# Attention values projected with 512 moving columns in place of 256

## The chip, the cores and the metric

One core of a Trainium2 chip runs the whole network in one launch. The metric is device time in microseconds. The engines are TensorE (PE, with its weight loads apart as PEld), VectorE (DVE), ScalarE (ACT), GpSimd (POOL) and SyncE (SP), which issues most DMAs here.

## The reference, cut to what matters

Four residual layers with token mixers A, B, C, A, each followed by a dense SwiGLU layer; 512 tokens, 1024 channels, float32. The change lies in mixer C, attention with three head groups of 16 heads (64 channels each) and dilations 1, 4 and 16:

```
qkv = (h @ w_qkv).reshape(b, s, N_ATTN_GROUPS, 3, HEADS_PER_GROUP, HEAD_DIM)
for g, (window, dil) in enumerate(DILATED_GROUPS):
    q = head_rms_norm(qkv[:, :, g, 0], q_gain[g])
    k = head_rms_norm(qkv[:, :, g, 1], k_gain[g])
    v = qkv[:, :, g, 2]
    o, l = dilated_group_attention(q, k, v, bias_g, dil, (window // 2) // dil)
wts = softmax(lses over the groups);  o = sum of wts * outs;  return o @ w_o
```

The values v have no norm of their own; the layer's norm is a factor per token.

## The kernel before, in words

The input of attention lies feature-major, as two float32r parts Hi and Lo whose sum is the value. A large product takes three matmuls per 128 rows of contraction: high by high, low by high, high by low. Weights come as chunks of 128 x 1024 in the order of their use (class Stream): SP loads a chunk into one of three raw buffers; ScalarE copies its high part (line 191), VectorE subtracts to get the low part (line 192), up to two chunks ahead of the use, each into rings of three. Loads wait on SP for a raw buffer, which comes free with the split.

Attention runs over n = 0 to 23: n // 3 is a pair of heads, n % 3 the group g. `gemm_qk(n, 0)` and `gemm_qk(n, 1)` make queries and keys of two heads with 24 matmuls of 512 columns (lines 332 to 334, stationary weights); VectorE scales the result by the norm (line 1397 and neighbours), ScalarE squares, VectorE rounds (line 1406), GpSimd takes the low part of the squares (line 1408). One step later `norms` sums the squares on TensorE (lines 1417, 1418) and ScalarE takes the root; `normed` scales on VectorE (line 1428). `score` (line 1450) follows one step after that, `soft` (VectorE 1464, ScalarE 1469), `divide` (GpSimd 1481), then `transposes` (TensorE 1503, copies out on ScalarE and VectorE 1505) and, four steps after the start, `pv` (TensorE 1518, 1522), the product of probabilities and values.

`gemm_v` makes the values of four heads of one group, tokens on the partitions: here the activations are stationary and the weights move. Group 0 takes 128 tokens in order; groups 1 and 2 take every fourth token, a stationary operand with a stride (`tok`, lines 1350 and 1351). It has four token tiles of 256 columns, two to a PSUM bank, and two weight chunks of four contraction tiles each, 96 matmuls (lines 1375 to 1377) in all. The copies out are two on VectorE (line 1381) and two on ScalarE (line 1383). In the loop it stands at the end of an iteration, for four heads per call: group 0 at n = 2, 8, 14, 20; group 1 at n = 3, 9, 15, 21; group 2 at n = 4, 10, 16 and, for the last heads, in the tail after the loop, before `score(22)`.

```
if 2 <= n < N - 2 and (n - 2) % 6 < 3:
    gemm_v((n - 2) // 6, (n - 2) % 6)
```

Between the parts of an iteration stand four `slot()` calls. Each takes the next closure of a list: after every four heads `merge_weights` (transposes of the logarithms, a softmax over three groups, a round trip through DRAM that copies a row to 64 partitions) and `merge_outputs` (GpSimd scales by these weights, line 1583; VectorE adds, lines 1587 and 1588). The program order within each engine's queue is the order in the code. PSUM has two rings of four banks: `psg` ("pg") for the large products and norms, `pst` ("pt") for scores, transposes and `pv`.

After the loop the last heads' steps are written out by hand, with the output projection (`project`, operand OH) in between.

Of the kernel before, what the change touches and what calls it, by code (L numbers as in the profile page):

```python
# [34 lines left out]
# ---------------------------------------------------------------- host layout  # L35
# [10 lines left out]
def _constants():  # L46
# [18 lines left out]
    # positions 2u and 2u + 1 against the frequencies to 128, and the position 256  # L65
# [39 lines left out]
def _host_arrays(v):  # L105
# [24 lines left out]
    w = v["attn_w_qkv"][0].reshape(KT, P, 3, 3, 4, 256)[:, :, :, 2]  # L130
    w = w.reshape(2, 4, P, 3, 4, 256)
    a["wv"] = cc(w.transpose(4, 3, 0, 2, 1, 5)).reshape(4, 3, 2, P, CH)
# [21 lines left out]
# ---------------------------------------------------------------- the program  # L154
class Stream:
    """Weight chunks in the order of their use. They are loaded ahead into a ring of
    buffers; those of the large products are split into two float32r parts, w = hi + lo
    exactly, one chunk ahead of their use."""
# [6 lines left out]
    def _room(self, tag, free):  # L165
        """Is the buffer that comes next in the ring given back?"""
        r, n = self.rings[tag], WBUFS if tag == "wch" else HBUFS
        return len(r) < n or r[-n] < (self.nsplit if tag == "wch" and self.loaders[r[-n]][1] else free)
# [35 lines left out]
    def next(self, count=1, ahead=True):  # L204
        """The next chunks; those given out before are free."""
        n = self.nuse
        if ahead:
            self.ahead(count)
        else:
            self._load(n)  # L210
        self.nuse += count
        out = [self.tiles.pop(i) for i in range(n, n + count)]
        return out if count > 1 else out[0]


class Net:
# [45 lines left out]
    # ---- weights in order of use  # L262
    def loaders(self):
# [6 lines left out]
        for l, kind in self.plan:  # L270
# [25 lines left out]
            elif kind == "attn":  # L296
                for n in range(24):
                    add(a["wqk"][n // 3, n % 3, 0])
                    add(a["wqk"][n // 3, n % 3, 1])
                    if n >= 2 and (n - 2) % 6 < 3:  # L300
                        v = [a["wv"][(n - 2) // 6, (n - 2) % 6, c] for c in range(2)]
                        if n < 22:
                            for x in v:
                                add(x)
                for x in v:
                    add(x)
                for half, kp in [(h, k) for h in range(2) for k in range(3)] + [(0, 3), (1, 3)]:
                    add(a["wo"][half, kp])
# [5 lines left out]
    def run_bg(self, slots):  # L314
        """Background work, spread over the slots that are left."""
        self.due += len(self.bg0) / self.slots if slots > 1 else len(self.bg0)
        while self.bg and len(self.bg0) - len(self.bg) < self.due:
            self.bg.pop(0)()
# [5 lines left out]
    def keep_warm(self, count):  # L324
        """Matmuls without a use, so that TensorE's clock isn't halved by the wait that follows."""
        ps = self.psg.tile([P, S], F32, name="pg", tag="pg")
        for _ in range(count):
            self.nc.tensor.matmul(ps, self.r[:, 0:P], self.r, start=True, stop=True)
# [7 lines left out]
    def gemm(self, hi, lo, chunk=None, ps=None, ks=range(KT)):  # L336
        """The next chunk's 128 columns against all of hi + lo."""
# [7 lines left out]
    # ---- residual stream and norms  # L345
# [4 lines left out]
    def mirrored(self, m):  # L350
        """Places of H for the positions: those above 256 backwards, 512 - s at 256 + s."""
# [3 lines left out]
    def start(self, nxt):  # L355
        """The first layer's input, as it comes in."""
# [19 lines left out]
    def after_x(self, m, nxt, late=None, defer=False):  # L376
# [38 lines left out]
        else:  # L415
# [5 lines left out]
            if late:  # L421
                # high part on ScalarE; VectorE takes the next sum before it waits for that
# [10 lines left out]
    def next_h(self):  # L433
        """A second place for the next layer's input."""
# [17 lines left out]
    # ---- feed forward  # L452
# [44 lines left out]
    def split_mul(self, hi, lo, t1, t2):  # L497
        """hi + lo = t1 * t2."""
# [5 lines left out]
    # ---- Fourier mixing  # L504
    def fnet(self, l, nxt):
        nc, H, j = self.nc, self.H, l // 3
        with ExitStack() as st:
# [12 lines left out]
            # the positions s = 2u and 2u + 1, then 512 - s for the odd and for the even ones. Position  # L520
            # 256, in the place of 512, is not to be folded: its row is taken apart.
# [6 lines left out]
            # block by block as the input comes in, for the first three tiles of tokens; the last  # L528
            # tile's products then run beside the norm's factors
# [24 lines left out]
            # the factors of the mirrored positions, in their order; zero at the place of 512  # L554
# [10 lines left out]
            def middle(hf, last):  # L565
                """Position 256."""
# [17 lines left out]
            def spread(u, ps, c):  # L584
                """The frequencies above 128 from those below."""
# [30 lines left out]
            def product(m, c):  # L616
                """The mixed channels' product with 128 columns of the weights."""
# [80 lines left out]
    # ---- S5: constants from the parameters, kept in DRAM until layer 1  # L698
# [12 lines left out]
    def store_h(self, k):  # L711
        """Block k of x * gain to DRAM."""
        self.nc.sync.dma_start(self.HB[k], self.H[:, k, :])

    def load_u(self, k):
        """... and back with (channel in group, step in chunk) on the partitions."""
# [3 lines left out]
    def s5_prepare(self):  # L720
        """Closures that each issue a part of the preparation."""
# [52 lines left out]
        def pexp1(x, scale=1.0):  # L774
            """exp(scale * x), to float32's accuracy, begun: x = k ln 2 + r."""
# [44 lines left out]
        def factors1():  # L820
            """(exp(lambda dt) - 1) / lambda."""
# [20 lines left out]
        def factors3():  # L842
            """One chunk's turn back, for the shift of the states."""
# [166 lines left out]
    # ---- S5 mixing  # L1010
# [10 lines left out]
    def s5_phase(self, k):  # L1021
        """The angles' cosines and sines."""
# [6 lines left out]
    def s5(self, l, nxt):  # L1029
# [7 lines left out]
        with self.s5_pools as st:  # L1037
# [10 lines left out]
            # the norm's factors with (channel, step in chunk) on the partitions  # L1048
# [9 lines left out]
            # The chunks of the backward direction are taken in reverse, so that both directions' scans are  # L1058
            # one. 64 chunks and a zero for each group make the groups' scans one, too; their results,
            # a column on, are the states each chunk starts from.  # L1060
# [73 lines left out]
            def spare(k, name, bufs):  # L1134
                """The angles' buffers serve again once their scans are done."""
# [12 lines left out]
            def product(ps, g, yw, k):  # L1148
                """One group's outputs: from the chunk's own inputs and from the state before it."""
# [18 lines left out]
            def outputs(k, half):  # L1168
                """Half of the groups of two blocks, which run beside each other on TensorE's columns."""
# [6 lines left out]
            def outputs1(k):  # L1176
                """The last two blocks, one by one."""
# [9 lines left out]
            def features(k):  # L1187
                """The outputs of blocks k - 1 and k back to feature-major; GELU."""
# [87 lines left out]
    # ---- attention  # L1276
# [5 lines left out]
    def attn_prepare(self):  # L1282
        """Bias rows by offset, copied 128 times so that skewed reads give the bias tiles."""
# [22 lines left out]
        return [load, lambda: None, rows(0), rows(1), rows(2), st.close]  # L1306

# [13 lines left out]
    def attn(self, l, nxt):  # L1321
# [27 lines left out]
        # tile t of 128 tokens: in order for group 0, every fourth token for the others  # L1349
# [3 lines left out]
        def norm_cols():  # L1353
            """The norm's factors with tokens on the partitions."""
# [9 lines left out]
        def gemm_v(q, g):  # L1364
            v = p2.tile([P, 4, 256], F32, name=f"v{g}", tag=f"v{g}", bufs=1)
            pp = [self.psg.tile([P, 2, 256], F32, name="pg", tag="pg") for t in range(2)]
            for c in range(2):
                wh, wl = [t.rearrange("p (k c) -> p k c", k=4) for t in self.stream.next()]
                for t in range(4):
                    ps = pp[t // 2][:, t % 2]  # L1370
                    for k in range(4):
                        kk = 4 * c + k
                        x, y = tok(Hi[:, kk], g, t), tok(Lo[:, kk], g, t)
                        # one start per bank: it clears the whole bank's marks
                        mm(ps, x, wh[:, k], start=(kk == 0 and t % 2 == 0), stop=False, skip_group_check=True)  # L1375
                        mm(ps, y, wh[:, k], start=False, stop=False, skip_group_check=True)  # L1376
                        mm(ps, x, wl[:, k], start=False, stop=(kk == 7), skip_group_check=True)  # L1377
            for t in range(4):
                s = rc[:, int(g > 0), t:t + 1]
                if t < 2:  # L1380
                    V.tensor_scalar(v[:, t], pp[t // 2][:, t % 2], s, None, M)
                else:
                    A.activation(v[:, t], pp[t // 2][:, t % 2], AF.Copy, scale=s)
# [47 lines left out]
        def score(n):  # L1431
# [3 lines left out]
            # (rows, query tile, columns of p, first key)  # L1435
# [10 lines left out]
            # the two heads lie in different rows of the array, and go side by side  # L1446
# [61 lines left out]
        def pv(n):  # L1508
# [4 lines left out]
            for t in range(4):  # L1513
                for h in range(2):
                    hc = slice(64 * (2 * (hp % 2) + h), 64 * (2 * (hp % 2) + h) + 64)
# [13 lines left out]
        def spread(copy, out, ps, g):  # L1529
            """From a group's order of the tokens to theirs."""  # L1530
# [9 lines left out]
        def merge_weights(q):  # L1540
            lr = p2.tile([P, 3, S], F32, name="lr", tag="mrg")[0:4]
            mxx = p2.tile([4, S], F32, name="mxx", bufs=1)
# [49 lines left out]
        # the output projection, in chunks of two k-tiles and four m-tiles  # L1592
# [22 lines left out]
        for n in range(N - 1):  # L1615
# [19 lines left out]
            if 2 <= n < N - 2 and (n - 2) % 6 < 3:  # L1635
                gemm_v((n - 2) // 6, (n - 2) % 6)
        # the last heads, with the output projection's products for the others between them
# [8 lines left out]
        gemm_v(3, 2)  # L1646
# [55 lines left out]
    # ---- all layers  # L1702
# [50 lines left out]
```

## Time and profile before

| | us |
|---|---|
| median of 3 runs (2568.99 to 2569.63) | 2569.31 |
| span of the profiled execution (first to last instruction), its own time as far as the profile gives one | 2565.2 |
| attention, about 1084 to 1786 of the span | 702 |
| one call of `gemm_v`, group 0 | 11.5 |
| one call of `gemm_v`, group 1 or 2 | 22.5 |

The profile has one execution: times are microseconds from the span's start. A matmul's end is modelled, so the spacing of starts tells its cost, not its length. "Idle before" and the releaser say how long an engine stood before an instruction and what ended that.

### The profile page before, as it was taken

Reading aid. Unit: us, or ns where it says so; the run is one execution under the profiler, and the core shown is the slowest. Engines: PE = TensorE matmul, PEld = TensorE weight load, DVE = VectorE, ACT = ScalarE, POOL = GpSimd, SP = SyncE. Lnnn points to the kernel's source line nnn. Section 1 sums busy time; section 2 is a strip of 40 time slices with the busy share of each in tenths; the row PEclk is TensorE's granted clock in tenths of the full one; section 3 lists DMA queues with packets and bytes.
Section 4 is the critical chain, followed back from the end, with each engine's and each line's share of the span. In section 5 each row is a group of like instructions: output and inputs, shape, how many; then the busy total and the mean of one; then the engine's idle time right before and its main releaser. Section 6 shows DMA issues by size and latency. Waiting matters only on the chain.

```text
span 2565.2 us, 31445 instructions
## 1 busy us (share of the span) xinstructions
PE 2446.1 (95%) x12330; PEld 2034.3 (79%) x12330; DVE 1394.7 (54%) x2143; ACT 871.8 (34%) x1515; POOL 629.6 (25%) x496
## 2 busy tenths in 40 slices
PE   9999978968998999999999999989999999999999
PEld 7777756857887787889888797877888888788887
DVE  7669999487542334462754646556433444543332
ACT  3322112434232223342644526354322322332231
POOL 4464554142110001121332323322110112310010
PEclk9999988989999999999999999999999999999999
DMA  4246876683226463322132322313322222222222
GB/s 148 91 138 208 243 208 193 209 287 118 97 102 100 122 128 118 108 75 66 58 91 66 91 66 66 91 50 91 107 99 99 98 93 97 85 96 99 99 98 83
DMA packets 137944, 293.80 MB, mean 115 GB/s; under 512 B 32449, under 2 KB 73508, under 8 KB 137796
## 3 DMA queue, kind: packets, MB, share of 16 engines
q1 hardware_dynamic: 136316, 288.09, 36.8%
q10 hardware_dynamic: 1480, 3.70, 0.5%
q8 instruction: 97, 1.59, 0.3%
q14 instruction: 51, 0.42, 0.1%
HBM read 259.66 MB, written 36.21 MB: 115 GB/s over the span
## 4 chain that ended last, share of the span: by engine, by line
PE 72%; DVE 15%; ACT 5%; DMA 3%; issue 3%; POOL 3%; SPq 0%; ACTq 0%; DVEq 0%; POOLq 0%
PE pg L332 19%; PE pg L334 19%; PE pg L333 19%; DVE wlo L192 3%; PE pg L1377 2%; PE pg L1376 2%; PE pg L1375 2%; DMA w<-in_wdn_dram 1%; ACT whi L191 1%; DMA w<-in_wgu_dram 1%; DVE s5bd L733 1%; ACT p L1469 1%; DVE wout L733 1%; DVE ce L733 1%; DVE ms L1115 1%
## 5 line engine op out<-in xcount | busy, mean ns | idle before, releaser
L192 DVE TENSOR_TENSOR wlo<-w,whi 128x1024 fp32r<-128x1024 f32 x360 | 484.1, 1348 | 613.3 <-ACT whi L191 606.4
L334 PE MATMUL pg<-HH,wlo 128*128 128x512 f32 x1792 | 709.7, 396 | 40.7 <-DVE wlo L192 40.7
L332 PE MATMUL pg<-HH,whi 128*128 128x512 f32 x1792 | 715.0, 399 | 7.9 <-ACT whi L191 4.5
L333 PE MATMUL pg<-HH,whi 128*128 128x512 f32 x1792 | 707.4, 395 | 2.1 <-DVE HH L419 2.1
L191 ACT CAST whi<-w 128x1024 fp32r<-128x1024 f32 x360 | 376.2, 1048 | 583.0 <-PE pg L333 408.6
L334 PEld LDWEIGHTS pg<-HH,wlo 128*128 128x128 f32 x1792 | 342.1, 191 | 118.7 <-DVE wlo L192 46.2
L332 PEld LDWEIGHTS pg<-HH,whi 128*128 128x128 f32 x1792 | 342.8, 191 | 88.0 <-ACT whi L191 5.7
L333 PEld LDWEIGHTS pg<-HH,whi 128*128 128x128 f32 x1792 | 342.4, 191 | 75.2 <-DVE HH L419 4.5
L502 POOL TENSOR_TENSOR act<-t,act 128x512 fp32r<-128x512 f32 x88 | 116.2, 1321 | 937.0 <-ACT act L501 889.3
L332 PE MATMUL pg<-act,whi 128*128 128x512 f32 x704 | 276.1, 392 | 11.0 <-ACT whi L191 10.5
L333 PE MATMUL pg<-act,whi 128*128 128x512 f32 x704 | 275.5, 391 | 1.6 <-POOL act L502 1.6
L334 PE MATMUL pg<-act,wlo 128*128 128x512 f32 x704 | 275.3, 391 | 0.0
L332 PEld LDWEIGHTS pg<-act,whi 128*128 128x128 f32 x704 | 132.9, 189 | 40.7 <-ACT whi L191 10.9
L333 PEld LDWEIGHTS pg<-act,whi 128*128 128x128 f32 x704 | 133.0, 189 | 30.4 <-POOL act L502 3.0
L334 PEld LDWEIGHTS pg<-act,wlo 128*128 128x128 f32 x704 | 132.8, 189 | 28.3 <-DVE wlo L192 0.8
L477 DVE TENSOR_TENSOR t<-pg,r 128x512 f32<-128x512 f32 x88 | 60.5, 688 | 166.9 <-PE pg L334 166.9
L1408 POOL TENSOR_TENSOR qsl<-qsq,qsh 128x512 fp32r<-128x512 f32 x48 | 63.1, 1315 | 310.3 <-DVE qsh L1406 271.7
L475 ACT ACTIVATE t<-t 128x512 f32<-128x512 f32 x88 | 55.6, 632 | 245.7 <-DVE t L474 240.2
L1375 PE MATMUL pg<-whi,HH 128*128 128x256 f32 x384 | 138.3, 360 | 0.0
L1377 PE MATMUL pg<-wlo,HH 128*128 128x256 f32 x384 | 137.5, 358 | 0.0
L1376 PE MATMUL pg<-whi,HH 128*128 128x256 f32 x384 | 137.5, 358 | 0.0
L501 ACT CAST act<-t 128x512 fp32r<-128x512 f32 x88 | 54.6, 621 | 221.9 <-DVE t L500 221.9
(331 smaller groups left out, 3181.4 us busy)
## 6 DMA issues: line engine op xcount, KB each, us to landing
w<-in_wgu_dram SPq DMA_DIRECT2D x176, 512.0 KB, 3.3
w<-in_wdn_dram SPq DMA_DIRECT2D x88, 512.0 KB, 3.3
w<-in_wqk_dram SPq DMA_DIRECT2D x48, 512.0 KB, 3.3
w<-in_wv_dram SPq DMA_DIRECT2D x24, 512.0 KB, 3.2
xpw<-s5SC SPq DMA_DIRECT2D x16, 512.0 KB, 7.4
xbj<-in_bj_dram SPq DMA_DIRECT2D x16, 512.0 KB
s5WE<-wout SPq DMA_DIRECT2D x16, 512.0 KB, 5.0
s5YW<-ce SPq DMA_DIRECT2D x16, 512.0 KB, 6.7
```

The lines of the kernel that those rows point to most:

```text
L191: nc.scalar.copy(hi, t)
L192: nc.vector.tensor_tensor(lo, t, hi, ALU.subtract)
L332: mm(ps, wh, hh, start=first, stop=False)
L333: mm(ps, wh, hl, start=False, stop=False)
L334: mm(ps, wl, hh, start=False, stop=last)
L477: nc.vector.tensor_tensor(t2, pp[1], self.r, ALU.mult)
L502: nc.gpsimd.tensor_tensor(lo, t1, hi, ALU.subtract)
L733: e.tensor_tensor(o, x, y, op)
L1375: mm(ps, x, wh[:, k], start=(kk == 0 and t % 2 == 0), stop=False, skip_group_check=True)
L1376: mm(ps, y, wh[:, k], start=False, stop=False, skip_group_check=True)
L1377: mm(ps, x, wl[:, k], start=False, stop=(kk == 7), skip_group_check=True)
L1408: G.tensor_tensor(sl, sq, sh, SB)
```

## The change

Groups 1 and 2 get their values for eight heads at a time. A call then has 512 moving columns, one token tile to a PSUM bank (four banks), and four weight chunks of two contraction tiles each: again 96 matmuls. There are two such calls per group, at n = 3 and 15 (group 1) and n = 4 and 16 (group 2); the calls at n = 9, 10, 21 and in the tail go. Group 0 stays as it was. The weights lie in DRAM in two arrays in the new order, the two value tiles grow from 4 to 8 KB per partition, and the tile of the merge's maximum moves to a buffer of the pool `work` that feed-forward layers use for squares. Comments are left out of the diff, as are the lines where only comments differ.

```diff
-    a["wv"] = cc(w.transpose(4, 3, 0, 2, 1, 5)).reshape(4, 3, 2, P, CH)
+    t = w[:, :, 0].reshape(2, 4, P, 4, 256)
+    a["wv0"] = cc(t.transpose(3, 0, 2, 1, 4)).reshape(4, 2, P, CH)
+    t = w[:, :, 1:].reshape(4, 2, P, 2, 2, 512)
+    a["wv12"] = cc(t.transpose(4, 3, 0, 2, 1, 5)).reshape(2, 2, 4, P, CH)
...
-                    if n >= 2 and (n - 2) % 6 < 3:
-                        v = [a["wv"][(n - 2) // 6, (n - 2) % 6, c] for c in range(2)]
-                        if n < 22:
-                            for x in v:
-                                add(x)
-                for x in v:
-                    add(x)
+                    q = self.v_group(n)
+                    if q:
+                        g, part = q
+                        for c in range(4 if g else 2):
+                            add(a["wv12"][part, g - 1, c] if g else a["wv0"][part, c])
...
+    def v_group(n):
+        if n >= 2 and (n - 2) % 6 == 0:
+            return 0, (n - 2) // 6
+        if n >= 2 and (n - 2) % 12 in (1, 2):
+            return (n - 2) % 12, (n - 2) // 12
...
-        def gemm_v(q, g):
-            v = p2.tile([P, 4, 256], F32, name=f"v{g}", tag=f"v{g}", bufs=1)
-            pp = [self.psg.tile([P, 2, 256], F32, name="pg", tag="pg") for t in range(2)]
-            for c in range(2):
-                wh, wl = [t.rearrange("p (k c) -> p k c", k=4) for t in self.stream.next()]
+        def gemm_v(g):
+            w = 512 if g else 256
+            kc, tb = CH // w, 512 // w
+            v = p2.tile([P, 4, w], F32, name=f"v{g}", tag=f"v{g}", bufs=1)
+            pp = [self.psg.tile([P, tb, w], F32, name="pg", tag="pg") for t in range(4 // tb)]
+            for c in range(KT // kc):
+                wh, wl = [t.rearrange("p (k c) -> p k c", k=kc) for t in self.stream.next()]
                 for t in range(4):
-                    ps = pp[t // 2][:, t % 2]
-                    for k in range(4):
-                        kk = 4 * c + k
+                    ps = pp[t // tb][:, t % tb]
+                    for k in range(kc):
+                        kk = kc * c + k
...
-                    hc = slice(64 * (2 * (hp % 2) + h), 64 * (2 * (hp % 2) + h) + 64)
+                    c0 = 64 * (2 * (hp % (4 if g else 2)) + h)
+                    hc = slice(c0, c0 + 64)
...
-            mxx = p2.tile([4, S], F32, name="mxx", bufs=1)
+            mxx = self.work.tile([P, S], F32, name="mxx", tag="sq", bufs=1)[0:4]
...
-            if 2 <= n < N - 2 and (n - 2) % 6 < 3:
-                gemm_v((n - 2) // 6, (n - 2) % 6)
+            q = self.v_group(n)
+            if q:
+                gemm_v(q[0])
...
-        gemm_v(3, 2)
```

## Rows read from the trace of the kernel before

**Rows 1.** The page: span, and busy time of TensorE

```profile
span 2565.2 us, 31445 instructions
...
PE 2446.1 (95%) x12330; PEld 2034.3 (79%) x12330; DVE 1394.7 (54%) x2143; ACT 871.8 (34%) x1515; POOL 629.6 (25%) x496
```

**Rows 2.** Waits of TensorE in attention, longest first: total us, times, longest

```profile
PE pg L334 <- DVE wlo L192: 8.8, 3, 2.9
```

**Rows 3.** Windows of the eight strided calls: busy us (instructions) by engine, clock

```profile
core 0: us, PE busy (x) PEld busy (x) DVE busy (x) ACT busy (x) POOL busy (x), PEclk, DMA share, GB/s
...
1311.05:1333.50 22.45, 22.45 (x99) 22.45 (x98) 10.95 (x11) 3.59 (x5) 9.13 (x4) 1.00 0.22 70
...
1693.30:1715.65 22.35, 22.35 (x97) 22.24 (x96) 9.99 (x10) 3.74 (x5) 7.03 (x4) 1.00 0.22 71
sum 179.75, PE 179.75 PEld 179.64 DVE 72.16 ACT 28.30 POOL 47.75; mean PE 22.47 PEld 22.45 DVE 9.02 ACT 3.54 POOL 5.97
```

**Rows 4.** Timeline of TensorE: start us, length, line, output<-inputs

```profile
1122.34 0.28 PE L1375 MATMUL pg<-whi,HH 128*128 128x256 f32 x1
1122.46 0.28 PE L1376 MATMUL pg<-whi,HH 128*128 128x256 f32 x1
...
1161.25 0.40 PE L1376 MATMUL pg<-whi,HH 128*128 128x256 f32 x1
1161.48 0.40 PE L1377 MATMUL pg<-wlo,HH 128*128 128x256 f32 x1
...
1171.29 0.39 PE L334 MATMUL pg<-HH,wlo 128*128 128x512 f32 x1
...
1176.06 0.39 PE L334 MATMUL pg<-HH,wlo 128*128 128x512 f32 x1
```

**Rows 5.** Timeline of weight loads, one moving column: first contiguous, then strided

```profile
1086.53 0.86 PEld L1359 LDWEIGHTS pt<-c_ones,acc 128*128 128x128 f32 x7 [0.24 <-issue]
...
1087.53 1.73 PEld L1359 LDWEIGHTS pt<-c_ones,acc 128*128 128x128 f32 x7
```

**Rows 6.** Windows of iterations 5 and 6, which have no value projection

```profile
1209.40:1225.40 16.00, 16.00 (x96) 12.88 (x96) 7.81 (x28) 10.61 (x29) 1.28 (x1) 1.00 0.10 34
1225.40:1242.00 16.60, 16.57 (x102) 13.31 (x101) 10.63 (x30) 10.72 (x29) 7.94 (x6) 1.00 0.19 63
```

**Rows 7.** Timelines of GpSimd and VectorE during the call of n = 9

```profile
1315.19 6.86 POOL L1583 TENSOR_TENSOR wb<-wb,og 128x1536 f32<-128x1536 f32 x2
...
1318.67 3.93 DVE L1587 TENSOR_TENSOR wb<-wb 128x512 f32<-128x512 f32 x1 [3.68 <-POOL wb L1583]
...
1323.24 2.35 DVE L192 TENSOR_TENSOR wlo<-w,whi 128x1024 fp32r<-128x1024 f32 x2
```

**Rows 8.** Timeline of VectorE in iteration 7, and the second addition at n = 10

```profile
1247.92 1.22 DVE L192 TENSOR_TENSOR wlo<-w,whi 128x1024 fp32r<-128x1024 f32 x1 [0.29 <-ACT whi L191]
...
1251.95 0.29 DVE L1464 CUSTOM_DVE_ANT_0 p<-pt,bias 128x128 f32<-128x128 f32 x1 [0.62 <-PE pt L1450]
...
1262.48 0.68 DVE L1505 COPY ptr<-pt 128x512 f32<-128x512 f32 x1
...
1341.99 0.68 DVE L1587 TENSOR_TENSOR wb<-wb 128x512 f32<-128x512 f32 x1
1342.71 1.65 DVE L1588 TENSOR_TENSOR OT<-wb 128x512 f32<-128x512 f32 x1
```

**Rows 9.** Timelines of TensorE, VectorE and GpSimd in the tail

```profile
1682.93 2.01 PE L1450 MATMUL pt<-tqk 64*128 64x256 f32 x20
...
1698.28 1.77 DVE L1428 SCALAR_TENSOR_TENSOR tqk<-tqk,c_kgain,qr 128x512 f32<-128x512 f32 x1
...
1699.47 5.18 POOL L1481 TENSOR_TENSOR pz<-pz,rd 128x1024 f32<-128x1024 f32 x2
...
1715.67 1.16 PE L1450 MATMUL pt<-tqk 64*128 64x128 f32 x16
```

**Rows 10.** Window at the start of iteration 9, where TensorE waits for a split

```profile
1290.30:1297.00 6.70, 3.73 (x9) 2.71 (x10) 6.68 (x5) 2.60 (x4) 2.56 (x1) 0.75 0.30 92
```

More of the change, by code (lines that the diff above doesn't have):

```diff
@@ L129, in _host_arrays @@
     a["wqk"] = cc(w[:, :, :, :2].transpose(4, 2, 3, 1, 0, 5)).reshape(8, 3, 2, P, CH)
-    w = v["attn_w_qkv"][0].reshape(KT, P, 3, 3, 4, 256)[:, :, :, 2]
-    w = w.reshape(2, 4, P, 3, 4, 256)
-    a["wv"] = cc(w.transpose(4, 3, 0, 2, 1, 5)).reshape(4, 3, 2, P, CH)
+    w = v["attn_w_qkv"][0].reshape(KT, P, 3, 3, D)[:, :, :, 2]
+    t = w[:, :, 0].reshape(2, 4, P, 4, 256)
+    a["wv0"] = cc(t.transpose(3, 0, 2, 1, 4)).reshape(4, 2, P, CH)
+    t = w[:, :, 1:].reshape(4, 2, P, 2, 2, 512)
+    a["wv12"] = cc(t.transpose(4, 3, 0, 2, 1, 5)).reshape(2, 2, 4, P, CH)
     w = v["attn_w_o"][0].reshape(4, 2, P, 2, 4, P).transpose(3, 0, 2, 1, 4, 5)
@@ L1306, in attn_prepare @@
         return [load, lambda: None, rows(0), rows(1), rows(2), st.close]
+    @staticmethod
+    def v_group(n):
[3 more added lines that the diff above has]
+            return (n - 2) % 12, (n - 2) // 12
     def bias_tile(self, pool, hp):
@@ L1362, in norm_cols @@
             return rc
-        def gemm_v(q, g):
-            v = p2.tile([P, 4, 256], F32, name=f"v{g}", tag=f"v{g}", bufs=1)
-            pp = [self.psg.tile([P, 2, 256], F32, name="pg", tag="pg") for t in range(2)]
-            for c in range(2):
-                wh, wl = [t.rearrange("p (k c) -> p k c", k=4) for t in self.stream.next()]
+        def gemm_v(g):
[5 more added lines that the diff above has]
+                wh, wl = [t.rearrange("p (k c) -> p k c", k=kc) for t in self.stream.next()]
                 for t in range(4):
-                    ps = pp[t // 2][:, t % 2]
-                    for k in range(4):
-                        kk = 4 * c + k
+                    ps = pp[t // tb][:, t % tb]
+                    for k in range(kc):
+                        kk = kc * c + k
                         x, y = tok(Hi[:, kk], g, t), tok(Lo[:, kk], g, t)
-                        mm(ps, x, wh[:, k], start=(kk == 0 and t % 2 == 0), stop=False, skip_group_check=True)
+                        mm(ps, x, wh[:, k], start=(kk == 0 and t % tb == 0), stop=False, skip_group_check=True)
                         mm(ps, y, wh[:, k], start=False, stop=False, skip_group_check=True)
-                        mm(ps, x, wl[:, k], start=False, stop=(kk == 7), skip_group_check=True)
+                        mm(ps, x, wl[:, k], start=False, stop=(kk == KT - 1), skip_group_check=True)
             for t in range(4):
                 s = rc[:, int(g > 0), t:t + 1]
+                i = pp[t // tb][:, t % tb]
                 if t < 2:
-                    V.tensor_scalar(v[:, t], pp[t // 2][:, t % 2], s, None, M)
+                    V.tensor_scalar(v[:, t], i, s, None, M)
                 else:
-                    A.activation(v[:, t], pp[t // 2][:, t % 2], AF.Copy, scale=s)
+                    A.activation(v[:, t], i, AF.Copy, scale=s)
             Vt[g] = v
```

## The prediction, made before the changed kernel was run

> **What bounds the kernel now.** I read the busy shares first, then the stage of the change by itself, then single matmuls. TensorE is busy 95% of the span [rows 1], but matmuls are pipelined, so that figure alone says little. The list of waits of the attention stage (1084 to 1786 us) says more: the longest sum of TensorE's waits there is 8.8 us in three waits [rows 2]. In some 700 us of attention TensorE is thus nearly always supplied, and whatever shortens its instruction stream shortens the span until another engine comes late.
>
> The stage holds 12 calls of the value projection, each 96 matmuls of 256 columns. The four of group 0 read their stationary operand contiguously; the eight of groups 1 and 2 take every fourth token. The strided ones fill 179.75 us of TensorE in eight windows at full clock, 22.47 us each [rows 3]. In the timeline the contiguous matmuls stand 0.12 us apart, the strided ones 0.233 us for the same 256 columns, and 512-column matmuls with a contiguous stationary operand (1171.29 to 1176.06, 21 matmuls) 0.227 us [rows 4]. So 256 columns more cost 0.227 - 0.120 = 0.107 us, and a strided call isn't bound by its columns. The norm's small products show by what: with one moving column, loads of contiguous weights follow each other at (0.86 - 0.19) / 6 = 0.112 us, strided ones at (1.73 - 0.33) / 6 = 0.233 us [rows 5] (0.19 and 0.33 us is one load). One column or 256, the strided spacing is 0.233 us: the weight load sets it, and the columns lie beneath it.
>
> **The change part by part.**
>
> *Wider calls.* Removed: eight strided calls, 768 loads, 179.75 us [rows 3]. Added: four calls of 96 matmuls with 512 columns, 384 strided loads. No row has a strided load with 512 columns. Lower bound: the larger of the load's 0.233 and the columns' 0.227 us [rows 4, 5]. Upper bound: load and columns in series, 0.233 + 2 x 0.107 = 0.446 us. I take 0.233, since going from 1 to 256 columns added nothing, and 512 still fit beneath the load. 384 x 0.233 = 89.6 us, so TensorE is relieved of 90.1 us. Group 0 is untouched; the number of weight chunks (24), their loads and their splits are the same, only in another order, and a wide call takes a chunk each 5.6 us, as the query/key products do.
>
> *Iterations that lose their call.* Calls stay at n = 3, 4, 15, 16, with twice the heads. Those at n = 9, 10, 21 and in the tail go. The windows of iterations without one (n = 5, 6) show what is left: 16.0 to 16.6 us, TensorE full, VectorE busy 7.8 to 10.6 us [rows 6]. So a bare iteration is covered, if nothing else comes. At n = 9 and 21 something does, the merge of four heads' outputs. GpSimd runs its two scalings for 6.86 us from 1315.19; VectorE, in program order, stands until the first is done, needs 3.93 us for an addition beside the second, and comes to its next weight split at 1323.24 [rows 7]. Today this lies beside the call that starts at 1311.05 and lasts 22.45 us [rows 3]. In the new order iteration 10 starts at 1311.05. By the pattern of n = 7, VectorE goes from a split's start to the softmax's first operation in 4.03 - 0.62 = 3.4 us (the 0.62 is a wait), and from there to the end of the last copy of transposed probabilities in 1262.48 + 0.68 - 1251.95 = 11.2 us; the second addition of the merge puts 2.4 us between (1341.99 to 1344.36) [rows 8]. So the copy for n = 7's heads is done at 1323.24 + 3.4 + 2.4 + 11.2 = 1340.2. TensorE would ask for it after iteration 10 (16.4 us) and one query product (24 x 0.227 = 5.5), at 1333.0. It waits 7.2 us there, and I put down 2.4 more (bounds 0 and 5) for the lag still in the following scores and norms: 9.6 us. n = 21 has the same pattern and runs into the tail: 7.2 us, and the following lag is in the next term. At n = 15 the call stays, but the third chunk's low half is split at 1323.24 + 1.2, by analogy 13.4 us after the call's start [rows 7], where the wide call wants it after 48 x 0.233 + 0.5 = 11.7: 1.7 us.
>
> *The tail.* The last narrow call (1693.30 to 1715.65, [rows 3]) stands before the scores of n = 22. Their last input, VectorE's scaling of k, is done at 1698.28 + 1.77 = 1700.05 [rows 9]. The gap is 6.75 us, measured from the last query/key product's end, and since TensorE and VectorE both hang on the same preceding scores (1682.93), it stays when all moves forward. GpSimd's division (5.18 us from 1699.47, [rows 9]), which today lies under the call, then meets the softmax of n = 22 on VectorE: one of its two operations, 2.5 us, between 0 and 5. After that the stretch is a chain of VectorE and ScalarE as now and moves as a block.
>
> *Clock.* After the stall that exists at n = 9 the granted clock averages 0.75 of full over 6.7 us [rows 10], so about half of that stretch is at 1.2 GHz; that gives back at most 1.7 us. Three new stalls of some 7 us: 4 us (0 to 8).
>
> *Costed at nothing.* A wide call takes all four banks of the products' ring instead of two. The fourth bank is first written 18 x 0.233 = 4.2 us after the start, and the operation that empties it takes 1.1 us right after the product; the first bank is complete 4.2 us before the call's end. If that cover went, up to 1 us per call. Copies out of PSUM are four of 512 columns for eight of 256, beside the call. The other place of the merge's maximum tile has no user within attention. SP's queue keeps its order but for the moved chunks.
>
> *Sum.* -90.1 + 9.6 + 7.2 + 1.7 + 6.75 + 2.5 + 4 = -58.3 us. The profile's span is 2565.2 us [rows 1], the only time that the profile gives of its execution; the median of the runs is 2569.3, 4.1 above. 2565.2 - 58.3 + 4.1 = 2511 us.
>
> **Rivals.**
>
> A. *The cover holds.* VectorE makes up its lag as it does in bare iterations, and only the tail's gap and n = 15 come back: -90.1 + 6.75 + 1.7 = -81.7, 2487.6 us. For it: n = 5 to 7 run bare with hardly a wait. Against it: none of them has a merge.
>
> B. *Load and columns partly in series.* If the 0.233 us of a narrow matmul were 0.126 of load and 0.107 of columns, a wide one would take 0.126 + 0.213 = 0.339, a call 32.5 us: 130.2 - 179.75 = -49.6; with the 31.8 us of new waits, 2551 us. Against it: the one-column loads at 0.233 [rows 5], which would have to agree by chance (they are of plain float32).
>
> C. *Slower.* A strided load that can't start until the array has streamed the matmul ahead of it: 0.446 us, 171.3 us in all. TensorE then gains 8.4 us and the new waits cost 31.8: +23.4, 2593 us. It decides from a spacing of (179.75 - 31.8) / 384 = 0.385 us upward. Against it: narrow strided matmuls would stand at 0.340, and they stand at 0.233 [rows 4], so it gets a small chance. The Trainium skill's "TensorE: Matmul & The Clock Gate" (section "The mechanism"), has such a rule: a weight load overlaps matmuls in flight only where their row groups differ, and here all use every row. By that rule the trace should show 0.112 + 0.107 = 0.219 us for contiguous narrow matmuls; it shows 0.12, so the rule doesn't hold for these rows.
>
> D. *The wide product isn't one instruction.* Were 512 columns issued as two matmuls with a load each, nothing would be saved: +31.8, 2601 us. Against it: the query/key products of 512 columns are single instructions [rows 4].
>
> **How the numbers follow.** Chances: forecast 0.75, A 0.12, B 0.07, C 0.04, D 0.02. The forecast's own range is 2490 to 2536: the lag terms run from a third of what I put (-80 with the clock's 4 at 0) to nearly double (-33). With A inside, and half-way to B, I give 2485 to 2541. No change means within 0.2%, 5.1 us, about what a measurement of this kernel can tell. Faster holds the forecast, A, and B: 0.94; slower C and D and a remainder: 0.05; same 0.01.
>
> **What would show it.** In the new profile: 384 strided matmuls of 512 columns at 0.233 us (0.34 is B, 0.45 is C), four windows of 22.4 us; iterations 10 to 12 and 22 with waits of TensorE on VectorE's copies or GpSimd's low parts of the squares of 6 to 8 us; a gap of some 7 us ahead of the scores of n = 22; everything outside attention unchanged. The prediction is wrong in its main step if the spacing is over 0.25 us, and in its second if the waits add to under 10 or over 50 us.

## The result, and the profile after

The changed kernel takes 2508.34 us (median of four runs, 2507.0 to 2513.11) against 2569.15 us for the kernel before (2568.32 to 2569.63). The ratio is 0.9767, interval 0.9753 to 0.9781: some 60.8 us less, where 58.3 were forecast.

The page after answers to [rows 1]; first the span, then busy time and instructions of each engine:

```profile
span 2511.3 us, 30661 instructions
...
PE 2372.4 (94%) x11946; PEld 1954.5 (78%) x11946; DVE 1393.0 (55%) x2135; ACT 870.9 (35%) x1507; POOL 627.4 (25%) x496
```

The matmuls fall from 12330 to 11946, exactly the 384 of the change. TensorE's busy time falls by 73.7 us but the span by 53.9. The profiled execution was the longest of the four, 2513.11 us, so the account below is made inside attention, from the first one-column product of the norm to the last product that reads OH: 698.0 us before (1086.53 to 1784.53), 636.4 us after (1088.78 to 1725.19), 61.6 us less. Outside it the profiled execution after was 7.7 us longer, in code that the change doesn't touch; some 5 us of it come in a stretch after attention whose granted clock was 0.66.

The four wide calls after, as windows (columns as in [rows 3]), with two short stretches that begin as a wait ends and the stretch after attention:

```profile
1150.81:1173.57 22.76, 22.76 (x100) 22.72 (x97) 9.86 (x11) 6.37 (x8) 2.69 (x3) 1.00 0.35 115
1189.67:1212.43 22.76, 22.76 (x99) 22.73 (x98) 10.19 (x10) 5.88 (x7) 2.90 (x3) 1.00 0.36 116
...
1442.70:1467.39 24.69, 23.23 (x100) 22.87 (x98) 13.90 (x13) 6.38 (x8) 9.25 (x4) 1.00 0.32 107
1483.47:1506.23 22.76, 22.76 (x100) 22.72 (x99) 10.53 (x10) 6.33 (x8) 3.83 (x4) 1.00 0.37 119
...
1342.40:1347.00 4.60, 4.58 (x22) 3.11 (x22) 3.45 (x4) 1.98 (x3) 1.28 (x1) 0.50 0.33 124
1655.40:1659.20 3.80, 3.75 (x22) 2.98 (x22) 1.61 (x12) 0.49 (x1) 3.76 (x3) 0.56 0.00 0
...
2090.00:2115.00 25.00, 22.92 (x101) 19.56 (x100) 11.96 (x26) 5.85 (x16) 6.65 (x3) 0.66 0.12 42
```

A wide call takes 22.76 us, hardly more than a narrow one took [rows 3], and there are four instead of eight. The third lasts 24.69: it holds a wait of its own.

TensorE's waits in attention after, longest first (total us, times, longest), to be held against [rows 2]:

```profile
PE pg L334 <- DVE wlo L194: 8.8, 3, 2.9
PE pt L1462 <- DVE tqk L1440: 7.5, 2, 6.5
PE pt L1531 <- ACT ptr L1517: 5.9, 1, 5.9
PE pg L1429 <- DVE qsh L1418: 5.5, 1, 5.5
...
PE pg L1388 <- DVE wlo L194: 1.5, 1, 1.5
```

The first line is the old one, unchanged. The four others are new (of the second, 1.1 us was there before), and each has its place in TensorE's timeline after (start, length, line, output<-inputs; in brackets the idle time ahead of it and what ended it):

```profile
1155.01 0.40 PE L1388 MATMUL pg<-wlo,HH 128*128 128x512 f32 x1
1155.25 0.40 PE L1386 MATMUL pg<-whi,HH 128*128 128x512 f32 x1
...
1342.41 2.55 PE L1531 MATMUL pt<-ptr,v 128*64 128x128 f32 x16 [5.94 <-ACT ptr L1517]
1344.90 0.80 PE L1429 MATMUL pg<-qsh,bonesr 128*128 128x512 f32 x1
...
1456.28 0.62 PE L1388 MATMUL pg<-wlo,HH 128*128 128x512 f32 x1 [1.46 <-DVE wlo L194]
...
1635.80 0.80 PE L1429 MATMUL pg<-qsh,bonesr 128*128 128x512 f32 x1 [5.48 <-DVE qsh L1418]
...
1655.45 2.08 PE L1462 MATMUL pt<-tqk 64*128 64x128 f32 x16 [6.47 <-DVE tqk L1440]
```

1342.41 lies in iteration 11, 1456.28 in the wide call of iteration 15, 1635.80 in iteration 23, and 1655.45 is the gap in the tail. The first pair shows a wide matmul every 0.24 us. The matmul behind the 5.94 us is slow itself (2.55 us for sixteen, the norm's 0.80 for one; 0.40 at full clock): the granted clock is 0.50 there, the 1.2 GHz level.

What keeps VectorE stands in the timelines of VectorE, GpSimd and ScalarE after:

```profile
1318.74 6.89 POOL L1596 TENSOR_TENSOR wb<-wb,og 128x1536 f32<-128x1536 f32 x2
...
1322.23 3.95 DVE L1600 TENSOR_TENSOR wb<-wb 128x512 f32<-128x512 f32 x1 [3.69 <-POOL wb L1596]
...
1326.83 1.22 DVE L194 TENSOR_TENSOR wlo<-w,whi 128x1024 fp32r<-128x1024 f32 x1
...
1330.35 1.61 POOL L1420 TENSOR_TENSOR qsl<-qsq,qsh 128x512 fp32r<-128x512 f32 x1 [4.71 <-PE pt L1515]
...
1341.26 0.63 ACT L1416 ACTIVATE qsq<-tqk 128x512 f32<-128x512 f32 x1 [3.07 <-DVE tqk L1409]
1341.80 0.57 ACT L1517 COPY ptr<-pt 128x512 f32<-128x512 f32 x1
...
1342.27 0.68 DVE L1517 COPY ptr<-pt 128x512 f32<-128x512 f32 x1
...
1653.64 1.75 DVE L1440 SCALAR_TENSOR_TENSOR tqk<-tqk,c_kgain,qr 128x512 f32<-128x512 f32 x1
1654.81 4.18 POOL L1493 TENSOR_TENSOR pz<-pz,rd 128x1024 f32<-128x1024 f32 x2
...
1658.53 0.50 DVE L1479 TENSOR_SCALAR ng<-mx 128x4 f32<-128x4 f32 x1
```

The first three lines are the merge at iteration 10, the stretch of [rows 7] again: VectorE idle for 3.69 us, then 3.95 us for an addition. TensorE's products at 1342.41 need two copies: ScalarE's at 1341.80, which ended the wait and stands in its queue behind squares that waited 3.07 us for VectorE, and VectorE's own at 1342.27. So both hang on VectorE. GpSimd's own queue isn't what is late: after the scalings it stands idle for 4.71 us. The last three are the tail.

### The profile page after: what moved, and what is told of

It is laid out like the page before. It is cut to its first block, busy times and chain, and to the rows that moved or that the text cites. A ratio compares the mean times of both kernels' runs of the same rounds, so it can differ in the third digit from the quotient of the medians.

```text
span 2511.3 us, 30661 instructions
## 1 busy us (share of the span) xinstructions
PE 2372.4 (94%) x11946; PEld 1954.5 (78%) x11946; DVE 1393.0 (55%) x2135; ACT 870.9 (35%) x1507; POOL 627.4 (25%) x496
## 4 chain that ended last, share of the span: by engine, by line
PE 67%; DVE 16%; ACT 7%; DMA 4%; issue 3%; POOL 3%; ACTq 0%; DVEq 0%; SPq 0%; POOLq 0%
PE pg L334 19%; PE pg L332 19%; PE pg L333 19%; DVE wlo L194 3%; ACT p L1481 1%; DMA w<-in_wdn_dram 1%; DMA w<-in_wgu_dram 1%; ACT whi L193 1%; PE pg L1388 1%; PE pg L1386 1%; PE pg L1387 1%; DVE s5bd L733 1%; DVE wout L733 1%; DVE ce L733 1%; PE pt L622 1%
## 5 line engine op out<-in xcount | busy, mean ns | idle before, releaser
L332 PEld LDWEIGHTS pg<-act,whi 128*128 128x128 f32 x704 | 133.2, 189 | 41.2 <-ACT whi L193 10.9
L398 POOL TENSOR_TENSOR acc<-acc,sq 128x512 f32<-128x512 f32 x42 | 62.6, 1491 | 238.3 <-ACT sq L393 238.0
L490 DVE TENSOR_TENSOR X<-X,pg 128x512 f32<-128x512 f32 x64 | 43.8, 685 | 89.9 <-PE pg L334 89.9
L1416 ACT ACTIVATE qsq<-tqk 128x512 f32<-128x512 f32 x48 | 30.3, 631 | 181.2 <-DVE tqk L1409 117.0
```

What stands on the lines that cost most here:

```text
L332: mm(ps, wh, hh, start=first, stop=False)
L398: eng.tensor_tensor(self.acc, self.acc, sq, ALU.add)
```

## Experiments

Times in the text below are medians; before was 2568 to 2571 us in every job. Theory: the wide call is bound by the strided load and saves four calls; some 27 us come back because those calls were cover for VectorE and GpSimd.

The changed kernel was not run again beside the experiments, so a difference of medians from it is one between jobs. Attention alone, taken in each profile between the same two instructions as above, is the steadier measure:

```
attention, us:  before 698.0   after 636.4
1: 617.3   2: 634.6   3: 702.1   4: 634.1   5: 624.6
6: 634.8   7: 621.9   8: 663.5   9: 618.2   10: 625.2
```

### 1. The narrow calls with a short stride (from the kernel before)

```diff
+        def tok_v(ap, g, t):
+            if g == 1:
+                return ap[:, 256 * (t // 2) + t % 2:256 * (t // 2) + 256:2]
+            return ap[:, P * t:P * t + P]
...
-                        x, y = tok(Hi[:, kk], g, t), tok(Lo[:, kk], g, t)
+                        x, y = tok_v(Hi[:, kk], g, t), tok_v(Lo[:, kk], g, t)
```

> The kernel before with one edit: the value projection of group 1 takes every second token of a block of 256 (stride 2) and that of group 2 takes 128 tokens in order (stride 1), so these values belong to other tokens than the reference's. Still eight narrow calls of 256 columns in the old places. Theory (the strided weight load sets a narrow matmul's spacing): the group 2 calls fall from 22.5 to 11.5 us, spacing 0.12 as in group 0; if stride 2 is as cheap as stride 1, group 1 does too and the time is about 2486 us (-88 of calls, +5 of waits where the third chunk's split is late at n = 9, 15, 21); if stride 2 costs like stride 4, about 2527. Rival (the narrow calls are slow because each matmul has too few columns or has some fixed cost, whatever the stride): all calls stay at 22.5 us, 2569.

Measured: 2485.29 us (2483.26 to 2487.95), ratio 0.9662 [0.9646, 0.9678]. TensorE's timeline, first a call with every second token, then one with adjoining tokens:

```profile
1150.49 0.28 PE L1381 MATMUL pg<-whi,HH 128*128 128x256 f32 x1
1150.62 0.28 PE L1382 MATMUL pg<-wlo,HH 128*128 128x256 f32 x1
...
1177.22 0.28 PE L1382 MATMUL pg<-wlo,HH 128*128 128x256 f32 x1
1177.34 0.28 PE L1380 MATMUL pg<-whi,HH 128*128 128x256 f32 x1
```

Both are spaced 0.12 to 0.13 us, and both kinds of call last 11.6 us instead of 22.47, with the same 256 columns. So the load's stride set the time of the narrow calls, as the prediction read it; and of the strides tried, that of two floats costs nothing and only that of four does. Eight calls at 10.9 us less are 87 us, of which 84 reach the end (2569.44 us for before in this job).

### 2. The wide calls with adjoining tokens (from the kernel after)

```diff
+        def tok_v(ap, g, t):
+            return ap[:, P * t:P * t + P]
...
-                        x, y = tok(Hi[:, kk], g, t), tok(Lo[:, kk], g, t)
+                        x, y = tok_v(Hi[:, kk], g, t), tok_v(Lo[:, kk], g, t)
```

> The changed kernel with one edit: the value projection of groups 1 and 2 takes 128 tokens in order in place of every fourth, so these values belong to other tokens. Theory (at 512 columns the strided load of 0.233 us lies beside 0.227 us of columns and shows only by what it is longer): the wide calls go from 22.76 to 21.8 us, 4 us in all, about 2504 us. Rival (load and columns are partly in series, so that the stride still costs at 512 columns): a loss of stride would give back 10 us or more per call.

Measured: 2504.83 us (2503.22 to 2506.44), ratio 0.974 [0.9726, 0.9754]. The window of its first wide call (22.76 us with the stride), which lasts 21.87 us in the timeline:

```profile
1148.90:1170.80 21.90, 21.90 (x102) 18.25 (x101) 10.46 (x11) 6.26 (x8) 3.31 (x3) 1.00 0.36 117
```

The weight loads' busy time drops from 22.72 to 18.25 us, the call's by 0.9. Without the stride 512 columns bind the call at 0.228 us a matmul; with it the load binds at 0.237. Were they in series as in rival B or C, taking the stride away would have saved 0.1 us or more per matmul, some 10 us per call. That refutes both. (Of the 3.6 us that the four calls give, attention shows 1.8, since the wait in the third grew by 2 us.)

### 3 and 4. The merge's additions three or four slots later (from before, and from after)

```diff
+            if q < 3:
+                return [lambda: scale(0), lambda: scale(1)] + [lambda: None] * 3 + [lambda: (add(0), add(1))]
             return [lambda: scale(0), lambda: (scale(1), add(0)), lambda: add(1)]
```

This takes away VectorE's standing in order behind the scaling at iterations 9, 15 and 21, which the prediction gave as the cause of the lag.

> The kernel before with the merge's closures in another order for the first three quarters of the heads: both scalings on GpSimd in their old slots, then three empty slots, then both additions on VectorE together at the end of iteration n = 10 (16, 22), so that VectorE no longer stands waiting for GpSimd. Theory (the value calls at n = 9 and 21 covered that wait): no change, 2569 within 3 us. Rival (VectorE's wait for GpSimd already cost something before): 5 us or more faster.

> The changed kernel with the same reordering of the merge's closures. Theory (TensorE's waits of 6.1 us at n = 11, 1.6 us at n = 15 and 5.6 us at n = 23, with slower matmuls after them, come from VectorE standing in its queue for GpSimd's scaling, then adding beside it): these waits mostly go, TensorE's spacing after them returns, and the time falls by 12 to 18 us to about 2493. Rival (a bare iteration's VectorE and ScalarE chain is too long with the additions wherever they stand): the waits move by an iteration and the gain is under 4 us.

Measured: from before 2573.07 us, ratio 1.001 [1.0001, 1.0018], so there is no gain where the calls are still cover; it is 3.6 us more, just outside the 3 allowed. From after 2505.55 us (2503.16 to 2507.26), ratio 0.9743 [0.9728, 0.9757]: 2.8 us less than after, not the some 15 that I expected. The rival's figures came instead: under 4 us, and waits that move. First a line of TensorE's waits from before with the edit, then three from after with it:

```profile
PE pt L1503 <- DVE mx L1464: 3.5, 2, 3.2
...
PE pt L1515 <- DVE mx L1476: 4.1, 1, 4.1
...
PE pt L1531 <- ACT ptr L1517: 2.4, 1, 2.4
...
PE pg L1429 <- DVE qsh L1418: 1.6, 1, 1.6
```

The waits of iterations 11 and 23 did fall, from 5.9 and 5.5 us to 2.4 and 1.6. But the additions, moved to the end of iteration 22, make TensorE's transposes after it wait 4.1 us, and those at iteration 10 put 1.9 us into iteration 11. The tail's new wait comes with the edit itself: it is there from before too (3.2 us at most, 1.5 in before), where attention grew by 4.1 us. So the small gain doesn't show that standing in order costs nothing: moving the additions is paid for elsewhere. VectorE and GpSimd at the same place show a second cause:

```profile
1317.70 7.92 POOL L1596 TENSOR_TENSOR wb<-wb,og 128x1536 f32<-128x1536 f32 x2
...
1317.79 4.47 DVE L194 TENSOR_TENSOR wlo<-w,whi 128x1024 fp32r<-128x1024 f32 x1 [0.29 <-ACT whi L193]
...
1324.03 1.88 DVE L1418 CAST qsh<-qsq 128x512 fp32r<-128x512 f32 x1 [0.76 <-ACT qsq L1416]
```

VectorE no longer waits for the scaling, but whatever it does beside it is stretched: the split takes 4.47 us instead of 1.22, a cast 1.88 where the median of 16 is 0.43. In after VectorE lost 7.0 us here, 3.69 of waiting and 3.27 in the stretched addition; now it loses 4.7, 3.25 in the split and 1.45 in the cast. The two scalings are longer as well, 7.92 us for 6.89. The Trainium skill's "SBUF — State Buffer" (section "Who interferes with whom") says that GpSimd's ports to the memory are also VectorE's second pair; these durations agree, as far as that two engines that run beside each other slow each other.

### 5. The merge's scaling on VectorE (from after)

```diff
-                e = V if q == 3 and i else G
+                e = V if q < 3 or i else G
```

The last quarter's first scaling stays on GpSimd.

> The changed kernel with the merge's two scalings on VectorE in place of GpSimd for all quarters (the additions in their old slots). The theory that VectorE's queue order causes the wait has fallen. Theory now (what delays VectorE at n = 9 to 11 and 21 to 23 is GpSimd's 7 us of scaling, beside which VectorE's operations on two SBUF operands take three to six times as long): VectorE does a scaling in 1.76 us, is through with the merge some 3 to 4 us earlier, TensorE's wait at n = 11 falls from 6.1 to about 3, that at n = 23 from 5.6 to about 2, that at n = 15 (1.6) goes; together with the spacing after them 8 to 12 us, about 2498 us. Rival (the merge's work as such is too much for a bare iteration, on whichever engine): waits unchanged, 2508, or longer, since VectorE gets 3.5 us more work each time.

Measured: 2495.01 us (2494.11 to 2497.47), ratio 0.9704 [0.9691, 0.9717], 13.3 us less than after (11.8 in attention) and within 3 of the expectation. VectorE, and the product of iteration 11 on TensorE:

```profile
1317.61 1.75 DVE L1596 TENSOR_TENSOR wb<-wb,og 128x1536 f32<-128x1536 f32 x1
...
1322.14 0.68 DVE L1600 TENSOR_TENSOR wb<-wb 128x512 f32<-128x512 f32 x1
...
1323.47 1.22 DVE L194 TENSOR_TENSOR wlo<-w,whi 128x1024 fp32r<-128x1024 f32 x1
...
1338.91 0.68 DVE L1517 COPY ptr<-pt 128x512 f32<-128x512 f32 x1
...
1339.07 0.32 PE L1531 MATMUL pt<-ptr,v 128*64 128x128 f32 x1 [2.26 <-ACT ptr L1517]
```

VectorE has more work and is done earlier: the addition takes 0.68 us instead of 3.95, and the copy that TensorE needs comes 3.4 us earlier. The wait in iteration 11 falls from 5.94 to 2.26 us, that of iteration 23 from 5.5 to 1.8, that of iteration 15 is gone, and the tail's gap falls from 6.47 to 5.0: some 10 of the 19 us of new waits. So about half of them hang on GpSimd's two scalings, which the narrow calls had covered. It also refutes the rival of experiments 4 and 5, that the merge is too much work for a bare iteration on whichever engine.

### 6 and 7. Group 0's call one iteration later (from after), and with experiment 5

```diff
-        if n >= 2 and (n - 2) % 6 == 0:
-            return 0, (n - 2) // 6
+        if n in (2, 9, 14, 21):
+            return 0, n // 6
```

It puts a call back where the merge runs. Experiment 7 has this and the edit of 5.

> The changed kernel with the second and fourth value call of group 0 (11.5 us each, contiguous) one iteration later, at n = 9 and 21 in place of 8 and 20. Theory (TensorE's waits at n = 11 and 23 are there because no call lies beside the merge any more; 11.5 us of cover are more than the 6 us missing): both waits go, with the slower spacing after them; 9 and 7 us, 2492 us, if the split waits of 5 us at the start of n = 9 and 21 stay as they are; up to 8 us of this is given back if those, which now have no call ahead of them, grow. Rival (VectorE's lag comes from iterations 10 and 22 themselves, which stay bare): waits unchanged, 2508.

> The changed kernel with both edits: the merge's scalings on VectorE and group 0's calls at n = 9 and 21. If both theories hold, n = 11 and 23 need no second remedy: the time is the call's move plus what the scaling gives at n = 15 alone (1.6 us and its clock), 2 to 4 us under the moved call alone, about 2489 us. Rival (two separate causes): the gains of the two edits add up.

Measured: 6 gave 2501.96 us (2501.03 to 2506.31), ratio 0.9733 [0.972, 0.9747], 10 us above what I expected, where up to 8 of loss had been allowed for; in attention it is only 1.7 us below after. Two products in its timeline say where it went:

```profile
1284.75 0.43 PE L1531 MATMUL pt<-ptr,v 128*64 128x128 f32 x2 [3.60 <-ACT ptr L1517]
...
1315.78 0.74 PE L334 MATMUL pg<-HH,wlo 128*128 128x512 f32 x1 [4.03 <-DVE wlo L194]
```

The waits in iterations 11 and 23 are gone, but iterations 8 and 20 now run bare: TensorE waits 3.6 us at 9 and 21, and the wait for a split, 2.9 us at most in after, is 4.03 us right behind the moved call. The cover was moved, not added. 7 gave 2494.24 us (2490.07 to 2499.64), the time of 5 within its spread. The same two products there:

```profile
1288.19 0.69 PE L1531 MATMUL pt<-ptr,v 128*64 128x128 f32 x2 [3.64 <-ACT ptr L1517]
...
1315.44 0.50 PE L334 MATMUL pg<-HH,wlo 128*128 128x512 f32 x1 [0.41 <-DVE wlo L194]
```

With the scalings on VectorE the wait behind the moved call is nearly gone, so an 11.5 us call didn't cover them; the wait at iteration 9 stays. In attention 7 gains 14.5 us on after, about the sum of 5's 11.8 and 6's 1.7, and 12.9 on 6, not the 2 to 4 expected. So 7 doesn't rule out the rival that the gains add: that both edits work on one cause is not shown.

### 8. Only group 1 wide (from after)

```diff
...
-        if n >= 2 and (n - 2) % 12 in (1, 2):
-            return (n - 2) % 12, (n - 2) // 12
+        if n >= 2 and (n - 2) % 12 == 1:
+            return 1, (n - 2) // 12
+        if n in (4, 10, 16):
+            return 2, (n - 2) // 6
...
-            w = 512 if g else 256
+            w = 512 if g == 1 else 256
...
         gemm_qk(N - 1, 1)
         divide(N - 3)
         normed(N - 2)
+        gemm_v(2)
```

> One part of the change alone: group 1 has two wide calls (n = 3, 15), group 2 keeps its four narrow calls (n = 4, 10, 16 and the tail). TensorE gets 89.9 - 45.5 = 44.4 us less to do. Theory (the new waits lie where a call that was cover is gone): no wait at n = 11, since the narrow call at the end of n = 10 is longer than the lag, and no gap of 6.7 us in the tail; the waits at n = 15 (1.6) and n = 23 (5.6) stay: 2.6 + 8 us given back, 2535 us. Rival (the new waits come with the wide call, by its four banks or its quicker chunks): n = 11 and the tail wait as in the changed kernel, about 2550 us.

Measured: 2532.75 us (2531.99 to 2535.36), ratio 0.9852 [0.9838, 0.9865]; 2535 was expected. TensorE's waits (lines are shifted by two to six):

```profile
PE pg L338 <- DVE wlo L196: 8.8, 3, 2.9
PE pg L1435 <- DVE qsh L1424: 5.5, 1, 5.5
...
PE pg L1394 <- DVE wlo L196: 1.5, 1, 1.5
```

With the narrow calls of iteration 10 and of the tail back, the waits of iteration 11 and of the tail are gone, and those of 15 and 23 stay to the tenth. Two calls fewer, 44.4 us, less these two waits with their slower matmuls, 9.6, are 34.8; attention is 34.5 us shorter than before (663.5 against 698.0). So the waits of iteration 11 and of the tail each belong to a missing call of group 2. That of 23 comes with group 1's change, which takes the call at 21 away (experiment 6, with a call back there, has no such wait), and that of 15 lies in the wide call itself.

### 9 and 10. The tail's block ahead (from 5), and 5 again beside it

```diff
         gemm_qk(N - 1, 0)
         norms(N - 2)
         score(N - 3)
...
+        normed(N - 2)
...
         divide(N - 3)
-        normed(N - 2)
```

VectorE scales the inputs of the scores of iteration 22 before TensorE's last query/key product instead of after it.

> The changed kernel with the merge's scalings on VectorE (the best so far) and one more edit in the tail: VectorE's scaling of the queries and keys of n = 22 is issued right after the softmax of n = 21, ahead of the weight split and the last keys' scaling, and no longer behind them. Theory (the tail's gap of 5 to 7 us ahead of the scores of n = 22 is there since their input stands in VectorE's queue behind a split that waits for ScalarE's exponentials and behind the last keys): the scores start at once after the last query/key product, the gap goes, and since the softmax of n = 22 still has to wait for VectorE some of it returns: 3 to 4 us faster than that kernel, about 2491.5 us. Rival (the tail is one chain of VectorE and ScalarE and the gap only shows where TensorE waits): the gap moves to the norms or scores of n = 23 and the time stays at 2495.

> The kernel with the merge's scalings on VectorE again, beside the kernel with the edit in the tail, so that the two share the runs of the kernel before: 2495 us within 3.

Measured in one job: 2489.24 us (2485.75 to 2493.48), ratio 0.969 [0.9672, 0.9708], against 2494.88 (2492.59 to 2495.93), ratio 0.9707 [0.9691, 0.9723]. The waits of the first:

```profile
PE pg L1429 <- DVE qsh L1418: 2.6, 2, 1.8
PE pt L1462 <- DVE tqk L1440: 2.5, 1, 2.5
```

The gap ahead of the scores of iteration 22, which in experiment 5 still measured 5.0 us, is gone; 2.5 are left ahead of those of iteration 23. So the gap hung on the order in VectorE's queue, and the rival, that it would only move, falls. The medians differ by 5.6 us (3 to 4 were expected; 7.0 in attention), and the runs of the two overlap only from 2492.59 to 2493.48. This version beats both kernels, the changed one by 19 us.

## Why the prediction was right

The time (2508.3 against 2511.0) and the mechanism came out. Terms of the sum, forecast and measured in the profile of after:

```
                                           forecast   measured
four wide calls for eight narrow ones        -90.1      -88.7
n = 11: the wait                               7.2        6.1
n = 21 to 23: the wait                         7.2        5.65
lag and slower clock after the waits       2.4 + 4        6.8
n = 15                                         1.7        1.9
gap in the tail                                6.75       6.65
GpSimd's division beside the softmax           2.5        0
smaller shifts (output projection, starts)     0         -0.1
sum                                          -58.3      -61.7
```

**The wide call.** 22.76 us over 96 matmuls is 0.237 us, not 0.233: 1.4 us too little in four calls. The choice of the lower bound was right, since experiment 2 shows how near the two limits lie and experiment 1 that the stride set the narrow spacing. Rival D falls with the count of 384 matmuls, rival A with the four new waits.

**The waits.** At n = 11 products wait 6.1 us in all on the copies of transposed probabilities, as described. At n = 23 it is 5.65, because half of the norms' inputs were there in time: only the second pair waited. The reason given for the lag was only part of it. The prediction named VectorE's standing in program order, and took the addition beside the second scaling at its 3.93 us without asking why it is so long. Experiment 4 took the standing away and gained 2.8 us, since the moved additions cost elsewhere; experiment 5 took GpSimd's work away from beside VectorE and gained 13.3. The term had the right size because its durations were read from a stretch where both were at work [rows 7]; how the lag divides between the two stays open.

**Clock and lag.** 3.2 us behind the wait of n = 11, 2.1 behind that of n = 23 and 1.5 behind the tail's gap are slower or later matmuls. Granted clock 0.50 and 0.56 in the two windows shows the 1.2 GHz level; the rows don't part it from the rest of the lag, and the forecast's 2.4 and 4 hold only as a sum.

**The tail.** The gap came as worked out from [rows 9]. The division term was wrong: GpSimd's two operations end at 1658.99, 1.4 us after the softmax begins, and of VectorE's operations in that time only one small one is longer (0.50 us at 1658.53, against 0.17 otherwise). The stretch from the end of the norms to the output projection took 11.00 us against 11.09.

**Costed at nothing.** Ring of banks, copies out of PSUM and weight chunks cost nothing that shows: three of the four calls run without a gap at 22.76 us.

**The chances.** C and D have 0.06 together, so "slower" had to be at least that; the 0.05 given is too little. The result doesn't hang on it.

## What to carry to other kernels

Hold the spacing of matmuls against the time of one load of their stationary operand: where the load is longer, more moving columns are free until they cover it, and a shorter stride, where the layout allows one, saves as much without any widening. A long run of matmuls is also cover for the other engines; before it is shortened, list what runs beside it, since each of three missing calls uncovered its own wait here, and nearly half of the time that came back hung on GpSimd's two scalings. Where VectorE is close to the path, count what it does beside GpSimd at the stretched durations, and try the work on VectorE itself. Work that is moved to another place lands beside something too: look what lies there first.

## What the runs showed of the hardware that was not expected

- A stationary operand of every second float loads as fast as adjoining ones (0.12 to 0.13 us between matmuls of 256 columns); every fourth takes 0.233.
- Loads and 512 columns overlap almost fully: 0.228 us with adjoining tokens, 0.237 with a load that alone needs 0.233.
- Beside a two-operand GpSimd operation VectorE's split took 4.47 us instead of 1.22, its addition 3.95 instead of 0.68, and a cast with one input 1.88 instead of 0.43. Two scalings took 6.89 us on GpSimd, and 1.75 us each on VectorE.
